# One factor of a gated recurrence, computed as (1 + a) times a root instead of as a root over (1 + a²)

## The chip, the cores and the metric

The kernel runs as one program on one core of a Trainium2 chip. The metric is the device time of one execution in microseconds; three executions of the kernel before are given, and their median counts. The engines are called TensorE (PE; PEld is its loading of weights), VectorE (DVE), ScalarE (ACT), GpSimd (POOL) and SyncE (SP), which here only issues DMAs.

## The reference

A model of two layers works on 256 context tokens and 256 latent tokens with 2048 features each. Every layer normalises, scales and shifts its input (`u`), multiplies it with one wide matrix `w_in`, gives the columns of the product to three mixers, and multiplies their gated results with `w_out`:

```
    u = rmsnorm(h, w) * (1 + scale) + shift
    lx, lg, q, k, v, ag, xbc, z, dt = split_cols(u @ w_in)
    h + gate * (concat([lru * silu(lg), att * silu(ag), ssd]) @ w_out)
```

`lru` is the mixer that the change is in, a gated linear recurrence over time, once forwards and once backwards, on 1024 columns; `att` is windowed attention with sinks; `ssd` is a chunked state-space mixer (Mamba-2), also in two directions. Of the recurrence, for one direction:

```
r = sigmoid(xc @ w_a + b_a);  i = sigmoid(xc @ w_x + b_x)      # xc: the column after a short convolution
log_a = -8 * r * softplus(-lambda)
a = exp(log_a)
b = sqrt(-expm1(2 * log_a)) * (i * xc)                         # sqrt(1 - a*a) * i * xc
h[t] = a[t] * h[t-1] + b[t]
```

## The kernel before, in words

**Projections.** Features lie on the 128 partitions, the 512 tokens in the free dimension. A projection's weights come in by DMA as pieces of four blocks of 128x128 (`raw`). ScalarE rounds a piece to TensorE's input format (`hi`, L237), VectorE subtracts that from the piece (`lo`, L238), and each block then takes three matmuls (`acc`, L174, called from `mm3`): `hi` with the rounded input, `hi` with the input's remainder, `lo` with the rounded input. So all three engines take part in every block, and TensorE works on blocks nearly all the time.

**The order of the work.** TensorE's order is fixed by the program as it is built: mixers are generators, and a planned clock that advances with each matmul says when a generator goes on (`spawn`, `pump`, and a table of waits by name and layer). The small matmuls of the mixers therefore stand among the blocks' matmuls at given places. All other engines are ordered by the compiler, which simulates a timeline and gives each engine a queue; a queue is worked off in order, and an instruction whose input is not ready holds up all behind it.

**The recurrence** (`lru_begin`, `lru_x`). There are eight column tiles `m` of 128 per layer, with two directions `d` each. For a tile, VectorE makes the convolution (`xc`, L466), ScalarE copies its halves over crosswise (`xsw`, L694), and TensorE multiplies with the gates' small matrices into two PSUM tiles (`mx`). ScalarE takes tanh of both with half the scale (L712, which frees the `mx` tiles; `lt0` is for r and `lt1` for i, since a sigmoid is (1 + tanh(z/2))/2). From `tr`, the tanh for r, come:

- L717: `tl` = tanh(log_a), where `s4` (-4 softplus) is both scale and bias, so that the argument is s4 (1 + tr) = log_a
- L718: `tr` becomes a = exp(log_a), in place
- L720: `a2` = a², a ScalarE square into a tile of its own (`la2`; the profile calls it `la`)
- L721: VectorE: `tl` = (1 + a²) tanh(log_a), which is a² - 1
- L722: VectorE: `ti` = (1 + ti) xc
- L724, once for both directions: `tl` = sqrt(-tl/16), in front of which ScalarE loads a table for the root
- L727, GpSimd, per direction: `ti` = `ti` times `tl`
- L730 (forwards), L733 and L735 (backwards, in two halves): the scans on VectorE; L739, GpSimd: the sum of the directions

**The state-space core.** Its steps run between those of the recurrence. `Output.begin` makes, per group of four heads, masked products (`cbm`, L1151), decays (`ee`: L1164 on ScalarE and L1165 on VectorE from `bc`, which a DMA broadcasts; the exponential at L1170), weights (`ww`, L1167 and L1168), their product (L1171), and `bc` likewise (L1175, L1176). `Output.end` multiplies `ee` with X and `bc` with the states H on TensorE into an `mx` tile and adds the result to Y (L1191, called X in the profile). The states are updated at L1119 to L1132.

**Tiles in rings.** Roles share buffers: `la2` is one of thirteen roles in a ring of four tiles of 128x512 (`xc`, the weighted X `xw` and the gates `lgt` are others). `mx` has four PSUM tiles, `acc` three.

Of the kernel before, what the change touches and what calls it, by code (L numbers as in the profile page):

```python
# [10 lines left out]
AF = mybir.ActivationFunctionType  # L11
ALU = mybir.AluOpType
AX = mybir.AxisListType

P = 128
# [124 lines left out]
class Kernel:  # L140
# [526 lines left out]
    def lru_begin(self, l):  # L667
        nc = self.nc
        o = PARAMS["lam"][0]
        ng = self.t([P, 16], "nlam", 1)  # L670
        nc.vector.tensor_scalar(out=ng, in0=self.prm[:, o:o + 16], scalar1=-1.0, scalar2=None, op0=ALU.mult)
        sp = self.softplus(ng, 16, "lsp")
        self.s4 = self.t([P, 16], "s4", 1)
        nc.vector.tensor_scalar(out=self.s4, in0=sp, scalar1=-4.0, scalar2=None, op0=ALU.mult)
        self.gb = self.t([P, 32], "gbh", 1)
        o = PARAMS["gab"][0]
        nc.vector.tensor_scalar(out=self.gb, in0=self.prm[:, o:o + 32], scalar1=0.5, scalar2=None, op0=ALU.mult)
        self.gws = [self.gate_weights(l, 0)]
        self.lruD = self.dram([8, P, 512], "lruD")
# [8 lines left out]
    def lru_x(self, l, m, px):  # L688
        nc = self.nc
        xc = self.t([P, 512], "xc")  # L690
        self.conv(xc, px, lambda tap: self.par("lcw", tap * 8 + m), self.par("lcb", m), 2)
        xs = self.t([P, 512], "xsw")
        for r, o in ((0, 64), (64, 0)):
            nc.scalar.activation(out=xs[r:r + 64], in_=xc[o:o + 64], func=AF.Copy)  # L694
        gw = self.gws.pop(0)
        if m < 7:
            self.gws.append(self.gate_weights(l, m + 1))
        yield self.wait("lx")
        ab = []
        tl = self.t([P, 2, 512], "ltl", 1)  # L700
        for d in range(2):
            if d:
                yield self.wait("lx2")
            th = []
            pg = [self.mx() for _ in range(2)]
            for r, c in ((0, 0), (64, 64), (0, 64), (64, 0)):
                x = xc if r == c else xs
                self.mm(pg[r // 64][c:c + 64], gw[r:r + 64, int(r != c), 2 * d + r // 64], x[r:r + 64], pos=(r, c),
                        side=4)
            for g in range(2):  # L710
                t = self.t([P, 512], f"lt{g}", 2)
                nc.scalar.activation(out=t, in_=pg[g], func=AF.Tanh, scale=0.5,  # L712
                                     bias=self.gb[:, 16 * g + 8 * d + m:16 * g + 8 * d + m + 1])
                th.append(t)
            tr, ti = th
            s4 = self.s4[:, 8 * d + m:8 * d + m + 1]
            nc.scalar.activation(out=tl[:, d], in_=tr, func=AF.Tanh, scale=s4, bias=s4)  # L717
            nc.scalar.activation(out=tr, in_=tr, func=AF.Exp, scale=s4, bias=s4)  # L718
            a2 = self.t([P, 512], "la2", 1)
            nc.scalar.activation(out=a2, in_=tr, func=AF.Square)  # L720
            nc.vector.scalar_tensor_tensor(out=tl[:, d], in0=a2, scalar=1.0, in1=tl[:, d], op0=ALU.add, op1=ALU.mult)  # L721
            nc.vector.scalar_tensor_tensor(out=ti, in0=ti, scalar=1.0, in1=xc, op0=ALU.add, op1=ALU.mult)  # L722
            ab.append((tr, ti))
        nc.scalar.activation(out=tl, in_=tl, func=AF.Sqrt, scale=-0.0625, bias=self.eps["s"])  # L724
        hs = []
        for d, (tr, ti) in enumerate(ab):
            nc.gpsimd.tensor_tensor(out=ti, in0=ti, in1=tl[:, d], op=ALU.mult)  # L727
            h = self.t([P, 512], f"lh{d}", 2)
            if d == 0:
                nc.vector.tensor_tensor_scan(out=h, data0=tr, data1=ti, initial=0.0, op0=ALU.mult, op1=ALU.add)  # L730
            else:
                r = lambda x, s: x[:, s:s + 256][:, ::-1]
                nc.vector.tensor_tensor_scan(out=r(h, 0), data0=r(tr, 0), data1=r(ti, 0), initial=0.0, op0=ALU.mult,  # L733
                                             op1=ALU.add)
                nc.vector.tensor_tensor_scan(out=r(h, C), data0=r(tr, C), data1=r(ti, C), initial=h[:, 0:1],  # L735
                                             op0=ALU.mult, op1=ALU.add)
            hs.append(h)
        s = C if l else 0
        nc.gpsimd.tensor_tensor(out=hs[0][:, s:], in0=hs[0][:, s:], in1=hs[1][:, s:], op=ALU.add)  # L739
        self.lru_h[m] = hs[0]  # L740
# [536 lines left out]
```

## Time and profile before

| what | value |
|---|---|
| three runs | 1833.20, 1832.97, 1830.13 us |
| median | 1832.97 us |
| the profiled execution | 1829.47 us |
| its span in the trace | 1827.5 us |
| mean granted TensorE clock | 0.991 |
| TensorE busy | 1765.5 us |

The profiled execution is one of its own, 3.5 us below the median; its span is the time from the first to the last record, and 2.0 us lie around it. The recurrence's tiles run at 240 to 500 us in the first layer and at 1255 to 1500 us in the second. Durations in the trace are those of one instruction, and successive ones on an engine overlap by about a tenth of a microsecond, so that what an instruction takes off an engine is a little less than its duration.

### The profile page before, as it was taken

How to read it: one execution, taken by the hardware profiler on the slowest of the kernel's cores; microseconds unless marked ns; L12 is line 12 of the kernel's file. 1: busy time of each engine (PE TensorE's matmuls, PEld its weight loads, DVE VectorE, ACT ScalarE, POOL GpSimd, SP SyncE). 2: the span in 40 equal slices, each digit the busy share in tenths (PEclk: the TensorE clock that was granted, in tenths of full speed). 3: DMA queues.
4: the chain of work that ended last, by engine and by line, in shares of the span. 5: the costliest groups of instructions: out<-in, count | busy, mean ns of one | idle time of the engine just before them, and what ended most of it. 6: DMA issues, size and time to landing. Idle time of an engine off the chain costs nothing.

```text
span 1827.5 us, 30170 instructions
## 1 busy us (share of the span) xinstructions
PE 1765.5 (97%) x10522; PEld 1453.4 (80%) x10522; DVE 1407.4 (77%) x3117; ACT 973.3 (53%) x1798; POOL 214.7 (12%) x179
## 2 busy tenths in 40 slices
PE   7999999999999999999999999999989999999999
PEld 4677876667778778887888887888767788999999
DVE  4447769898899778899999536877688785788665
ACT  4324578688523354556232235545688863678443
POOL 0000111111210021211000021010021130121000
PEclk9999999999999999999999999999999999999999
DMA  9982333434675545556766433455243564554655
GB/s 364 389 292 66 124 104 102 122 122 146 220 221 180 179 150 185 178 182 221 238 220 222 158 122 107 133 185 168 96 138 107 179 214 142 182 178 155 217 185 179
DMA packets 186344, 322.99 MB, mean 177 GB/s; under 512 B 19121, under 2 KB 44625, under 8 KB 185553
## 3 DMA queue, kind: packets, MB, share of 16 engines
q1 hardware_dynamic: 186192, 321.09, 54.2%
q8 instruction: 82, 1.34, 0.3%
q14 instruction: 70, 0.57, 0.1%
HBM read 310.38 MB, written 10.63 MB: 176 GB/s over the span
## 4 chain that ended last, share of the span: by engine, by line
PE 72%; DVE 9%; issue 7%; ACT 7%; DMA 3%; POOL 1%; SPq 0%; ACTq 0%; DVEq 0%; POOLq 0%
PE acc L174 55%; PE mx L174 13%; PE ada L174 3%; DVE lo L238 2%; PE mx L170 2%; DMA bc<-acsD 1%; ACT hi L237 1%; DVE ada L380 1%; DVE araw L380 1%; ACT lt L712 1%; DVE lh L730 1%; DMA araw<-in_adaw_dram 1%; DVE xc L466 1%; DVE ee L1165 1%; ACT ww L1167 1%
## 5 line engine op out<-in xcount | busy, mean ns | idle before, releaser
L174 PE MATMUL acc<-u,hi 128*128 128x512 f32 (+1 forms) x4800 | 1277.4, 355 | 3.9 <-ACT u L452 3.1
L174 PEld LDWEIGHTS acc<-u,hi 128*128 128x128 f32 x4800 | 837.1, 190 | 149.0 <-issue 32.6
L174 PE MATMUL acc<-u,lo 128*128 128x512 f32 (+1 forms) x2400 | 842.4, 351 | 6.9 <-DVE lo L238 6.7
L237 ACT ACTIVATE hi<-raw 128x512 fp32r<-128x512 f32 x640 | 397.8, 628 | 544.4 <-PE acc L174 420.8
L238 DVE TENSOR_TENSOR lo<-raw,hi 128x512 fp32r<-128x512 f32 x640 | 457.9, 718 | 184.6 <-ACT hi L237 172.7
L174 PEld LDWEIGHTS acc<-u,lo 128*128 128x128 f32 x2400 | 455.5, 190 | 71.9 <-DVE lo L238 11.7
L380 DVE SCALAR_TENSOR_TENSOR araw<-araw,adac 128x512 f32<-128x512 f32 x256 | 183.2, 716 | 6.9 <-DMA araw<-in_adaw_dram 4.1
L380 DVE SCALAR_TENSOR_TENSOR ada<-araw,adac 128x512 f32<-128x512 f32 x192 | 141.6, 738 | 13.0 <-DMA adac<-condD 7.0
L174 PE MATMUL mx<-u,hi 128*128 128x512 f32 (+1 forms) x320 | 99.7, 395 | 0.0
L1077 DVE SCALAR_TENSOR_TENSOR X<-acc,mod,X 128x256 f32<-128x256 f32 x144 | 65.0, 478 | 39.5 <-PE acc L174 39.4
L727 POOL TENSOR_TENSOR lt<-lt,ltl 128x512 f32<-128x512 f32 x32 | 45.5, 1443 | 326.2 <-ACT ltl L724 305.3
L868 POOL TENSOR_SCALAR prob<-prob,qrs 128x512 f32<-128x512 f32 (+1 forms) x48 | 58.2, 1227 | 214.7 <-ACT hi L237 124.7
L427 POOL TENSOR_TENSOR ssq<-ssq,sq 128x512 f32<-128x512 f32 (+1 forms) x26 | 34.1, 1312 | 308.0 <-ACT sq L423 308.0
L174 PEld LDWEIGHTS mx<-u,hi 128*128 128x128 f32 x320 | 56.6, 191 | 14.2 <-issue 4.6
L174 PE MATMUL mx<-u,lo 128*128 128x512 f32 (+1 forms) x160 | 61.0, 382 | 0.0
L511 POOL TENSOR_SCALAR X<-xs,prm 128x512 f32<-128x512 f32 (+1 forms) x16 | 15.4, 968 | 361.6 <-DVE xs L489 357.1
L174 PE MATMUL mx<-xc,gw 64*64 64x512 f32 x128 | 40.8, 619 | 8.9 <-ACT lt L712 5.9
L423 ACT ACTIVATE sq<-X 128x256 f32<-128x256 f32 (+1 forms) x44 | 18.8, 452 | 54.8 <-DVE X L654 53.1
L1165 DVE SCALAR_TENSOR_TENSOR ee<-bc,nacs,ee 128x128 f32<-128x128 f32 x96 | 35.9, 427 | 15.0 <-DMA bc<-acsD 9.6
L771 POOL TENSOR_TENSOR qw<-qw,cst 128x256 f32<-128x256 f32 x20 | 23.1, 1156 | 197.7 <-DVE rt L770 169.7
L712 ACT ACTIVATE lt<-mx,gbh 128x512 f32<-128x512 f32 x64 | 42.0, 674 | 4.1 <-PE mx L174 4.0
L1164 ACT ACTIVATE ee<-bc,nacs 128x128 f32<-128x128 f32 x96 | 30.9, 390 | 17.7 <-DMA bc<-acsD 17.7
(240 smaller groups left out, 1953.1 us busy)
## 6 DMA issues: line engine op xcount, KB each, us to landing
raw<-in_w_in_dram SPq DMA_DIRECT2D x448, 256.0 KB, 2.8
araw<-in_adaw_dram SPq DMA_DIRECT2D x256, 256.0 KB, 3.0
raw<-in_w_out_dram SPq DMA_DIRECT2D x192, 256.0 KB, 3.0
ar<-in_ada_dram SPq DMA_DIRECT2D x84, 256.0 KB, 5.4
bc<-acsD SPq DMA_DIRECT2D x48, 256.0 KB, 3.7
ar<-in_ada_dram SPq DMA_DIRECT2D x22, 512.0 KB, 6.9
adac<-condD SPq DMA_DIRECT2D x28, 256.0 KB, 4.5
gw<-in_gates_dram SPq DMA_DIRECT2D x16, 256.0 KB, 2.9
```

Source lines behind the costliest of these rows:

```text
L170: self.nc.tensor.transpose(out=out, in_=lhsT, identity=rhs)
L174: self.nc.tensor.matmul(out=out, lhsT=lhsT, rhs=rhs, start=start, stop=stop, **kw)
L237: nc.scalar.activation(out=hi, in_=part, func=AF.Copy)
L238: nc.vector.tensor_tensor(out=lo, in0=part, in1=hi.bitcast(F32), op=ALU.subtract)
L380: i = nc.vector.scalar_tensor_tensor(out=o, in0=raw, scalar=1.0, in1=row[c].rearrange("p t x -> p (t x)"), op0=ALU.mult, op1=ALU.mult, acc ...
L427: nc.gpsimd.tensor_tensor(out=self.ssq[0], in0=self.ssq[0], in1=sq, op=ALU.add)
L712: nc.scalar.activation(out=t, in_=pg[g], func=AF.Tanh, scale=0.5, bias=self.gb[:, 16 * g + 8 * d + m:16 * g + 8 * d + m + 1])
L727: nc.gpsimd.tensor_tensor(out=ti, in0=ti, in1=tl[:, d], op=ALU.mult)
L868: nc.gpsimd.tensor_scalar(out=pr[j], in0=pr[j], scalar1=rs[:, j:j + 1], scalar2=1.0, op0=ALU.mult, op1=ALU.mult)
L1077: nc.vector.scalar_tensor_tensor(out=x[:, s], in0=acc[:, s.start - w0:s.stop - w0], scalar=mod[:, 2 * KT + m, c:c + 1], in1=x[:, s], op0=A ...
L1164: nc.scalar.activation(out=e[:, j], in_=bcs[0][:, j], func=AF.Identity, bias=k.nacs[:, f:f + 1])
L1165: nc.vector.scalar_tensor_tensor(out=e[:, j], in0=bcs[1][:, j], scalar=k.nacs[:, r:r + 1], in1=e[:, j], op0=ALU.add, op1=ALU.min)
```

## The change

With T = tanh(log_a / 2) the identity sqrt(1 - a²) = (1 + a) sqrt(-T) is used in place of 1 - a² = -(1 + a²) tanh(log_a). A second scale `s2` of half the size is made once per layer. The square and its tile go; the multiply of VectorE stays in number, reads `a` in place of `a²`, and stands behind the root instead of ahead of it, once per direction and each just ahead of GpSimd's multiply. The root is still taken once for both directions. Behind the change, lines of `lru_x` up to the exponential have numbers higher by two: tanh of the gates is L714, the tanh 719, the exponential 720; VectorE's L722 becomes L721, the root L723, the multiply L726.

```
+        self.s2 = self.t([P, 16], "s2", 1)
+        nc.vector.tensor_scalar(out=self.s2, in0=sp, scalar1=-2.0, scalar2=None, op0=ALU.mult)
...
-            s4 = self.s4[:, 8 * d + m:8 * d + m + 1]
-            nc.scalar.activation(out=tl[:, d], in_=tr, func=AF.Tanh, scale=s4, bias=s4)
+            s4, s2 = (x[:, 8 * d + m:8 * d + m + 1] for x in (self.s4, self.s2))
+            nc.scalar.activation(out=tl[:, d], in_=tr, func=AF.Tanh, scale=s2, bias=s2)
             nc.scalar.activation(out=tr, in_=tr, func=AF.Exp, scale=s4, bias=s4)
-            a2 = self.t([P, 512], "la2", 1)
-            nc.scalar.activation(out=a2, in_=tr, func=AF.Square)
-            nc.vector.scalar_tensor_tensor(out=tl[:, d], in0=a2, scalar=1.0, in1=tl[:, d], op0=ALU.add, op1=ALU.mult)
             nc.vector.scalar_tensor_tensor(out=ti, in0=ti, scalar=1.0, in1=xc, op0=ALU.add, op1=ALU.mult)
...
         for d, (tr, ti) in enumerate(ab):
+            nc.vector.scalar_tensor_tensor(out=tl[:, d], in0=tr, scalar=1.0, in1=tl[:, d], op0=ALU.add, op1=ALU.mult)
             nc.gpsimd.tensor_tensor(out=ti, in0=ti, in1=tl[:, d], op=ALU.mult)
```

The orders of TensorE and of GpSimd are the same before and after. ScalarE has 32 instructions fewer, the squares, and 69 table loads either way; VectorE has two small ones more (`s2`, one per layer). In the orders that follow, a name is a tile with the number it got when it was made: `lt_592` before and `lt_590` after are the same tile, the second direction's `a`.

ScalarE before, in the second tile of the first layer, from the exponential of the second direction (L718) to the root (L724):

```order
L718 ACTIVATE lt_592_2838<-lt_592_2838,s_428_2078 128x512
L1164 ACTIVATE ee_2891<-bc_2887,nacs_2356 128x128 x4
L720 ACTIVATE la_594_2844<-lt_592_2838 128x512
L1167 ACTIVATE ww_2892<-cbm_2883,dt_2151 128x128 x4
L1167 ACTIVATE ww_2955<-cbm_2883,dt_2151 128x128 x4
L1175 ACTIVATE bc_2887<-bc_2887 128x512
L237 ACTIVATE hi_3037<-raw_3035 128x512
L1170 ACTIVATE ee_2891<-ee_2891 128x512
L724 ACT_TABLE_LOAD
L724 ACTIVATE ltl_2809<-ltl_2809,epss_92 128x1024
```

ScalarE after, the same place (exponential L720, root L723):

```order
L720 ACTIVATE lt_590_2833<-lt_590_2833,s_428_2078 128x512
L723 ACT_TABLE_LOAD
L723 ACTIVATE ltl_2807<-ltl_2807,epss_92 128x1024
L1164 ACTIVATE ee_2885<-bc_2881,nacs_2358 128x128 x4
L1167 ACTIVATE ww_2886<-cbm_2877,dt_2153 128x128 x4
L1167 ACTIVATE ww_2949<-cbm_2877,dt_2153 128x128 x4
L237 ACTIVATE hi_3031<-raw_3029 128x512
L1175 ACT_TABLE_LOAD
L1175 ACTIVATE bc_2881<-bc_2881 128x512
L1170 ACTIVATE ee_2885<-ee_2885 128x512
```

The table load and the root have moved up, past the steps of the state-space core, to right behind the exponential. A table load stands ahead of `bc`'s exponential (L1175) instead, since the root's table is in use until then.

VectorE before, the same place, from the first products `cbm` on:

```order
L1151 TENSOR_TENSOR cbm_2885<-mx_2881,cst_76 128x128
L1165 SCALAR_TENSOR_TENSOR ee_2891<-bc_2889,nacs_2356,ee_2891 128x128 x4
L721 SCALAR_TENSOR_TENSOR ltl_2809<-la_594_2844,ltl_2809 128x512
L1168 SCALAR_TENSOR_TENSOR ww_2892<-cbm_2885,dt_2151,ww_2892 128x128 x4
L1168 SCALAR_TENSOR_TENSOR ww_2955<-cbm_2885,dt_2151,ww_2955 128x128 x4
L1176 TENSOR_TENSOR bc_2887<-bc_2887,CT_1802 128x512
L238 TENSOR_TENSOR lo_3038<-raw_3035,hi_3037 128x512
L1191 TENSOR_TENSOR X_1805<-mx_2940,X_1805 128x2x128
L1171 TENSOR_TENSOR ee_2891<-ee_2891,ww_2892 128x512
```

VectorE after (L726 is the multiply behind the root):

```order
L1151 TENSOR_TENSOR cbm_2879<-mx_2875,cst_76 128x128
L726 SCALAR_TENSOR_TENSOR ltl_2807<-lt_586_2814,ltl_2807 128x512
L726 SCALAR_TENSOR_TENSOR ltl_2807<-lt_590_2833,ltl_2807 128x512
L1165 SCALAR_TENSOR_TENSOR ee_2885<-bc_2883,nacs_2358,ee_2885 128x128 x4
L1168 SCALAR_TENSOR_TENSOR ww_2886<-cbm_2879,dt_2153,ww_2886 128x128 x3
L730 SCALAR_TENSOR_TENSOR lh_592_2843<-lt_586_2814,lt_587_2816 128x512
L1168 SCALAR_TENSOR_TENSOR ww_2886<-cbm_2879,dt_2153,ww_2886 128x128
L1168 SCALAR_TENSOR_TENSOR ww_2949<-cbm_2879,dt_2153,ww_2949 128x128 x3
L733 SCALAR_TENSOR_TENSOR lh_593_2847<-lt_590_2833,lt_591_2835 128x256
L1168 SCALAR_TENSOR_TENSOR ww_2949<-cbm_2879,dt_2153,ww_2949 128x128
L238 TENSOR_TENSOR lo_3032<-raw_3029,hi_3031 128x512
L1176 TENSOR_TENSOR bc_2881<-bc_2881,CT_1802 128x512
```

Both multiplies stand one behind the other ahead of the decays `ee` (L1165), and the scans L730 and L733, which stood behind L1171 before, are among the weights `ww`. L1171 for `ee` follows three rows further on.

ScalarE before, in the last tile of the first layer, from the weights `ww` to the swapped halves `xsw`:

```order
L1164 ACTIVATE ee_4411<-bc_4407,nacs_2356 128x128 x4
L1167 ACTIVATE ww_4347<-cbm_4338,dt_2151 128x128 x4
L1167 ACTIVATE ww_4412<-cbm_4338,dt_2151 128x128 x4
L598 ACTIVATE spe_11776<-nlam_11774 128x16
L1175 ACTIVATE bc_4407<-bc_4407 128x512
L237 ACTIVATE hi_4541<-raw_4539 128x512
L694 ACTIVATE xsw_4301<-xc_4296 64x512 x2
```

ScalarE after, the same place:

```order
L1164 ACTIVATE ee_4389<-bc_4385,nacs_2358 128x128 x4
L696 ACTIVATE xsw_4279<-xc_4274 64x512 x2
L1167 ACTIVATE ww_4325<-cbm_4316,dt_2153 128x128 x4
L1167 ACTIVATE ww_4390<-cbm_4316,dt_2153 128x128 x4
L598 ACTIVATE spe_11746<-nlam_11744 128x16
L1175 ACTIVATE bc_4385<-bc_4385 128x512
```

The two copies to `xsw` stand ahead of the eight weights instead of behind them.

## Rows read from the trace of the kernel before

**Rows 1.** The page: engines, then the chain that ended last, by engine.

```profile
PE 1765.5 (97%) x10522; PEld 1453.4 (80%) x10522; DVE 1407.4 (77%) x3117; ACT 973.3 (53%) x1798; POOL 214.7 (12%) x179
...
PE 72%; DVE 9%; issue 7%; ACT 7%; DMA 3%; POOL 1%; SPq 0%; ACTq 0%; DVEq 0%; POOLq 0%
```

**Rows 2.** Busy us by engine (count), TensorE clock, DMA share, GB/s, of two stretches.

```profile
360.00:420.00 60.00, 55.53 (x303) 39.69 (x301) 55.32 (x112) 47.39 (x100) 8.28 (x6) 1.00 0.35 113
420.00:480.00 60.00, 57.59 (x298) 42.83 (x297) 55.49 (x123) 41.48 (x73) 11.12 (x8) 0.97 0.59 200
```

**Rows 3.** TensorE's waits, 222 to 500 us: total, times, longest.

```profile
PE mx L174 <- DVE ee L1171: 4.5, 2, 3.1
PE mx L174 <- ACT lt L712: 3.1, 1, 3.1
PE mx L174 <- DVE H L1132: 2.7, 1, 2.7
PE mx L174 <- ACT xsw L694: 2.3, 1, 2.3
```

**Rows 4.** TensorE's waits, 1225 to 1500 us.

```profile
PE mx L174 <- ACT lt L712: 9.7, 7, 4.1
PE acc L174 <- DVE lo L238: 4.7, 5, 1.6
```

**Rows 5.** Groups by form: count | busy, mean ns | idle before, releaser.

```profile
L238 DVE TENSOR_TENSOR lo<-raw,hi 128x512 fp32r<-128x512 f32 x640 | 457.9, 718 | 184.6 <-ACT hi L237 172.7 <-DMA ar<-in_ada_dram 5.5 <-PE acc L174 2.0
...
L727 POOL TENSOR_TENSOR lt<-lt,ltl 128x512 f32<-128x512 f32 x32 | 45.5, 1443 | 326.2 <-ACT ltl L724 305.3 <-DVE X L1191 20.9
...
L730 DVE TENSOR_TENSOR_SCAN lh<-lt,lt 128x512 f32<-128x512 f32 x16 | 29.0, 1813 | 8.9 <-POOL lt L727 8.9
...
L724 ACT ACT_TABLE_LOAD x16 | 20.5, 1283 | 0.3
...
L720 ACT ACTIVATE la<-lt 128x512 f32<-128x512 f32 x32 | 20.0, 628 | 0.6
...
L724 ACT ACTIVATE ltl<-ltl,epss 128x1024 f32<-128x1024 f32 x16 | 18.4, 1153 | 0.2
...
L733 DVE TENSOR_TENSOR_SCAN lh<-lt,lt 128x256 f32<-128x256 f32 x16 | 10.7, 672 | 0.0
```

**Rows 6.** ScalarE's waits, 222 to 500 us.

```profile
ACT xsw L694 <- DVE xc L466: 14.2, 5, 4.2
...
ACT ee L1164 <- DMA bc<-acsD: 8.7, 5, 2.7
```

**Rows 7.** VectorE's waits, 222 to 500 us.

```profile
DVE ltl L721 <- ACT la L720: 2.1, 4, 0.7
```

**Rows 8.** Timeline of ScalarE, second LRU tile: start us, us, operation [idle].

```profile
274.50 0.80 ACT L718 ACTIVATE lt<-lt,s 128x512 f32<-128x512 f32 x1
```

**Rows 9.** Timeline of VectorE, same stretch.

```profile
275.97 1.13 DVE L1165 SCALAR_TENSOR_TENSOR ee<-bc,nacs,ee 128x128 f32<-128x128 f32 x4
...
281.44 0.68 DVE L1171 TENSOR_TENSOR ee<-ee,ww 128x512 f32<-128x512 f32 x1
...
283.92 1.35 DVE L238 TENSOR_TENSOR lo<-raw,hi 128x512 fp32r<-128x512 f32 x1 [1.20 <-ACT hi L237]
```

**Rows 10.** Timeline of TensorE, around the second tile's SSD outputs.

```profile
283.89 0.45 PE L174 MATMUL mx<-ee,X 128*64 128x128 f32 x4
...
293.20 0.70 PE L174 MATMUL mx<-ee,X 128*64 128x128 f32 x4 [3.15 <-DVE ee L1171]
```

**Rows 11.** Busy time and clock of two short stretches.

```profile
292.40:299.20 6.80, 6.00 (x26) 4.84 (x27) 6.80 (x12) 2.74 (x8) 2.55 (x2) 0.50 0.19 67
...
442.60:446.00 3.40, 3.33 (x25) 2.91 (x24) 3.40 (x8) 3.31 (x7) 0.00 (x0) 0.50 0.57 178
```

**Rows 12.** Timeline of ScalarE, around 440 and 1415 us.

```profile
440.38 1.28 ACT L694 ACTIVATE xsw<-xc 64x512 f32<-64x512 f32 x2
...
1415.60 1.28 ACT L1175 ACT_TABLE_LOAD   x1
```

## The prediction, made before the changed kernel was run

> **What bounds the kernel now.** I read the page's engines first, then the chain, then a table of stretches, and only then waits and timelines. TensorE is busy for 97% of the span and leads the chain with 72%; VectorE (77% busy, 9% of the chain) and ScalarE (53%, 7%) come in only where TensorE waits for them [rows 1]. A ScalarE instruction less is therefore worth nothing by itself; it is worth what it takes out of TensorE's waits. The change lies in the recurrence's tiles, so the stretch decides, not the average: from 360 to 480 us VectorE is busy for 55.32 + 55.49 = 110.8 of 120 us, as close to the limit as TensorE (113.1), while ScalarE is busy for 88.9 [rows 2]. Here VectorE is the second engine at its limit, and ScalarE is not. TensorE's waits in the stretch are few and single: 4.5 us in two for `ee`'s product (L1171), 3.1 us in one for the gates' tanh, 2.7 us for H, 2.3 us for `xsw` [rows 3]; in the second layer 9.7 us in seven for the tanh and 4.7 us in five for `lo` [rows 4]. These sums, 12.6 and 14.4 us, are nearly all there is to gain. Some waits cost more than their length: behind that of 3.15 us [rows 10] the clock stands at 0.50 (1.2 GHz) for 6.8 us, and behind the one for `xsw` for 3.4 us [rows 11], which with TensorE busy in nearly all of it costs half of each, 3.4 and 1.7 us.
>
> **The change part by part.**
>
> *The squares.* Thirty-two of 628 ns, 20.0 us in all, leave ScalarE [rows 5]; since successive instructions overlap by a tenth, some 0.53 us each, 17 us. All of it lies beside TensorE's matmuls. VectorE waited for the squares for only 2.1 us in four times, at most 0.7 [rows 7], so even VectorE gains little from their going. Directly: 0. If the cover were gone, that is if ScalarE set the pace, it would be up to 17 us.
>
> *The second scale.* Two VectorE operations on 128x16, once per layer. No row shows their like alone; the nearest is the half scan of 128x256 at 672 ns [rows 5], so from 0 to 1.3 us on both, ahead of the first tiles. I take 0, for TensorE is in the projections there and VectorE is not at its limit. The tanh and the exponential keep their shapes, so 0.
>
> *The ring.* The square's tile no longer goes round in the ring of four. The squares idled 0.6 us in all before they started [rows 5], so they waited for no tile. The other roles of the ring may get theirs earlier, which is a gain from 0 to the 14.2 us that `xsw` waited for `xc` on ScalarE in the first layer [rows 6]. I take 0 for it: what stands ahead of `xc` on VectorE is other VectorE work.
>
> *The root moves up and VectorE's multiply moves behind it.* This is the part with a price. The multiply could run when the square was done; now it needs a table load (1283 ns) and a root of 1153 ns, 2.43 us, against 0.53 to 0.63 us for the last square. VectorE works its queue off in order, and behind the multiply stand `ee`, `ww` and L1171, for which TensorE has stood still before. In the second tile of the first layer I follow it through. The exponential starts at 274.50 and ends at 275.30 [rows 8], so load and root end at 275.30 + 2.43 = 277.7. VectorE reached `ee` (L1165) at 275.97 [rows 9]; now both multiplies stand ahead of it, so it idles 277.7 - 276.0 = 1.7 us. Ahead of L1171 there come further one multiply more (0.6), the scan L730 (0.5 to 1.8: its mean, 1813 ns, holds the longer ones beside GpSimd) and the half scan L733 (0.67) [rows 5], some 3.1 at most, and GpSimd's two multiplies of 1443 ns, which now lie beside all this: a `lo` in the shadow of one took 1.35 us [rows 9] against a mean of 0.72 [rows 5], and I put that down as 1.7 us on the stretch. L1171 ended at 281.44 + 0.68 = 282.1; now at 282.1 + 1.7 + 3.1 + 1.7 = 288.6. TensorE wanted it at 283.89 and did not wait [rows 10]: there was 1.8 us of slack, and there will be a wait of 288.6 - 283.9 = 4.7 us. For the next output, where it waited 3.15, the scans are now out of the way, and 0.6 us remain. Sum for the tile: 4.7 + 0.6 - 3.15 = +2.15 us. The clock falls once before and once after, so 0 for that. A second tile of the first layer has the same root ahead of the same product; its wait, 2.43 less a few tenths of slack, I take as +2.1 us. For the other six I take 0: there the root is done before VectorE comes to the multiply. Bounds: from 0 (root always in time) to 8 tiles by 1.7, 13.6 us; between them I stand at 4.25, nearest to the tile worked out.
>
> *ScalarE's other work shifts.* Moved up with the root, a few instructions of 0.53 us now stand ahead of the gates' tanh at two places, one in each layer: two each, +1.05 and +1.05, together +2.1 us. In the other direction: the second wait for L1171 (4.5 - 3.1 = 1.4) goes, -1.35. In the last tile of the first layer the copies to `xsw` ran at 440.38, behind eight weights [rows 12]; they stand ahead of them now, so of the wait of 2.3 us at least 0.9 goes, and with a wait of 1.4 I take it that the clock keeps its level (from 360 to 420 us, where the waits of 1.4 and 2.7 us lie, it is 1.00 throughout [rows 2, 3]), so -0.9 - 1.7 = -2.6. In the second layer, a table load of 1.28 us at 1415.60 [rows 12] no longer stands ahead of a tanh for which TensorE waits, and another wait is shorter by a square: -2.1. The longest wait there, 4.1 us, ended with a `bc` whose DMA stood behind a weight's on SyncE and does not any more: -1.0. Of the `lo` waits I take a square per two, -1.0. Bounds for these gains: 0, and all of rows 3 and 4, 27 us, less the waits for H.
>
> *Sum.* +4.25 + 2.1 - 1.35 - 2.6 - 2.1 - 1.0 - 1.0 = -1.7 us. From the profiled execution, 1829.47, that gives 1827.8; the runs' median is 3.5 us above that execution, so I add 3.5 and predict 1831 us. Against the median it is -0.1%. About 0.2%, 3.7 us, is what a measurement of this kernel tells from no change; the sum is under it.
>
> **GpSimd beside VectorE.** The row is the one above: a `lo` with two inputs in SBUF took 1.35 us while GpSimd multiplied, against 0.72 in the mean [rows 5, 9]. The Trainium skill, page "SBUF — State Buffer", section "Who interferes with whom", has a rule for it: a VectorE instruction with two SBUF inputs and a GpSimd instruction that reads SBUF take one pair of ports for a whole instruction, and the one that comes second waits for all of the other. That speaks against this change, since the second direction's multiply now stands in the queue exactly when GpSimd starts on the first direction's. By the rule it would wait for up to 1.44 us, sixteen times; by the row it would lose 0.63 us, sixteen times. In the sum neither stands: GpSimd multiplies 32 times before and after, and whichever VectorE instruction lies beside it pays.
>
> **The rivals.**
>
> *ScalarE's relief reaches TensorE (faster).* The waits for the tanh are 3.1 + 9.7 = 12.8 us [rows 3, 4], and 17 us leave ScalarE. If the tanh comes earlier at all of these places, the time is 1829.47 - 12.8 + 3.5 = 1820.2; at half of them, 1826.6. For it: the tanh is the second layer's largest wait. Against: ScalarE itself waits, 14.2 us for `xc` and 8.7 us for the DMA of `bc` in the first layer [rows 6]; time taken off ahead of such a wait only lengthens it, and the squares stand behind the tanh of their own tile.
>
> *VectorE is held by the root (slower).* One mechanism: a multiply at the head of VectorE's queue waits for table and root, and everything behind it comes late to TensorE. It decides where VectorE has less than the 1.8 us of slack that the second tile shows. Over 360 to 480 us it idles for 9.2 us, with four tiles in it [rows 2]. If four tiles pay 1.7 us and no gain elsewhere comes, the time is 1829.47 + 6.8 + 3.5 = 1839.8; with all eight, 13.6 us, 1846.6. By the rule on the ports each would add up to 1.44 us, the same rival and not one of its own. Against it: the compiler's order put the multiplies behind some other work in most tiles.
>
> *The change is not what moves the time.* The queues of ScalarE, VectorE and SyncE are made anew by the compiler, and what differs is mainly their order; table loads stay at 69. Then the time may come out anywhere within a few microseconds, 1833 in the middle.
>
> **How the numbers follow.** Waits trade places, the forecast: 0.52, with its own range from 1826 to 1837; of it 0.33 within 0.2%, 0.12 faster, 0.07 slower. ScalarE's relief: 0.22, all faster. VectorE held: 0.20, of it 0.18 slower and 0.02 within. Only the order: 0.06, with 0.02 faster, 0.03 within, 0.01 slower. Together: faster 0.36, within 0.38, slower 0.26. The range goes from the full relief, 1820, to just above four tiles held, 1842.
>
> **What would show it.** Right: in the profile after, ScalarE has 32 operations and some 20 us less in the recurrence; TensorE's waits there sum to about what they did, with a longer one for L1171's output near 284 us, and none or a short one for `xsw` near 440. VectorE's list of waits has a new row, the multiply for the root, of 1 to 2 us a time. Wrong to the fast side: the tanh's waits in the second layer fall below half of 9.7 us. Wrong to the slow side: the multiply waits for the root in most of the tiles and L1171 is late in more than two, or VectorE's longer operations beside GpSimd rise in number. If the waits are as now and the time differs, the clock's low stretches have to show it.

## The result: slower by 1.1%

| | median us | runs | ratio to before, 95% interval |
|---|---|---|---|
| before | 1831.55 | 4 (1829.46 to 1833.20) | |
| changed | 1851.98 | 4 (1845.10 to 1854.22) | 1.0108 [1.0093, 1.0123] |

The changed kernel takes 20 us more; the forecast was 1831, with a range to 1842. Its profiled execution took 1853.59 us, with a span of 1851.6, 24.1 us more than the one before.

The page of the changed kernel, the engines and the chain, beside [rows 1]:

```profile
PE 1777.0 (96%) x10522; PEld 1461.5 (79%) x10522; DVE 1412.1 (76%) x3119; ACT 959.5 (52%) x1766; POOL 221.4 (12%) x179
...
PE 76%; DVE 9%; ACT 8%; DMA 4%; issue 3%; POOL 0%; SPq 0%; ACTq 0%; DVEq 0%; POOLq 0%
```

ScalarE has its 32 squares less (1766 operations against 1798), and 13.8 us less to do. The time shows none of it: TensorE has the same 10522 matmuls and is busy for 11.5 us more, which goes with the lower clock (below), and the rest is waiting.

TensorE's waits in the first and the second layer's recurrence (in total, times, longest), from 222 to 520 and from 1225 to 1540 us, beside [rows 3] and [rows 4]; in these somewhat longer stretches the rows before that are compared here have the same numbers:

```profile
PE mx L174 <- DVE ee L1171: 9.5, 5, 4.4
PE mx L174 <- ACT lt L714: 4.1, 2, 3.8
```

```profile
PE acc L174 <- DVE lo L238: 9.1, 6, 2.0
PE mx L174 <- ACT lt L714: 7.9, 5, 3.9
PE acc L174 <- ACT hi L237: 5.0, 4, 1.9
```

In the first layer the waits for L1171's product are five instead of two, 9.5 us against 4.5. In the second the tanh's waits are shorter, 7.9 against 9.7, as ScalarE's relief would have it; but the waits for `lo` have doubled from 4.7 to 9.1 us, and waits for `hi`, of which there was none before, make 5.0. VectorE's list has the new row that the prediction named, here for both layers:

```profile
DVE ltl L726 <- ACT ltl L723: 13.5, 8, 2.5
```

```profile
DVE ltl L726 <- ACT ltl L723: 12.3, 8, 2.5
```

Sixteen waits, once per tile, 25.8 us in all. The clock, beside [rows 11], in two stretches of the second layer (columns as there):

```profile
1447.60:1454.40 6.80, 5.09 (x14) 3.67 (x15) 6.80 (x9) 4.79 (x10) 2.80 (x2) 0.50 0.35 115
1502.20:1509.00 6.80, 5.77 (x27) 5.77 (x28) 6.80 (x10) 3.01 (x5) 2.12 (x2) 0.50 0.50 162
```

TensorE's gaps of more than 0.3 us and the time at a clock of 0.50, summed over the trace's records for the two profiled executions:

| | gaps before | gaps after | clock at 0.50 before | after |
|---|---|---|---|---|
| 222 to 520 us | 14.2 | 19.8 | 13.7 | 13.7 |
| 1225 to 1540 us | 15.6 | 23.4 | 3.4 | 23.9 |
| all | 56.3 | 68.9 | 35.4 | 61.4 |

Twelve and a half microseconds more of gaps, and 26 us more at half the clock, worth 13: 25.6 us for the span's 24.1. Since TensorE's order is the same in both, its instructions can be laid side by side one by one: the changed kernel is 0.9 us behind at 240 us of the one before, 5.8 at 490, 8.3 at 1225 and still at 1300, and 23.7 at 1530. So a third of the loss lies in the first layer and two thirds in the second, where the prediction had seen a gain.

**What happens in the second layer.** ScalarE, VectorE and GpSimd of the changed kernel at the first of the places (start us, us, operation, [idle before]):

```profile
1328.45 0.81 ACT L720 ACTIVATE lt<-lt,s 128x512 f32<-128x512 f32 x1
1329.26 1.28 ACT L723 ACT_TABLE_LOAD   x1
1330.55 1.15 ACT L723 ACTIVATE ltl<-ltl,epss 128x1024 f32<-128x1024 f32 x1
1331.61 0.61 ACT L237 ACTIVATE hi<-raw 128x512 fp32r<-128x512 f32 x1
1332.13 0.76 ACT L460 ACTIVATE xc<-acc,prm 128x512 f32<-128x512 f32 x1
```

```profile
1331.73 1.29 DVE L726 SCALAR_TENSOR_TENSOR ltl<-lt,ltl 128x512 f32<-128x512 f32 x2 [1.86 <-ACT ltl L723]
1332.94 1.76 DVE L238 TENSOR_TENSOR lo<-raw,hi 128x512 fp32r<-128x512 f32 x1
```

```profile
1332.51 3.34 POOL L727 TENSOR_TENSOR lt<-lt,ltl 128x512 f32<-128x512 f32 x2 [11.28 <-DVE ltl L726]
```

And TensorE there:

```profile
1332.27 0.51 PE L174 MATMUL acc<-u,hi 128*128 128x256 f32 x2 [1.67 <-ACT hi L237]
1334.76 0.41 PE L174 MATMUL acc<-u,lo 128*128 128x256 f32 x1 [1.98 <-DVE lo L238]
```

Table load and root stand right behind the exponential, and the next `hi` behind them, 2.4 us of load and root later: TensorE waits 1.67 us for it. VectorE has nothing to do in the meantime but its multiplies, since `lo` needs `hi`, and waits 1.86 us for the root; then it runs both, 1.29 us, ahead of `lo`. The first multiply's end starts GpSimd, and `lo` lies beside it and takes 1.76 us. TensorE waits another 1.98 us for that `lo`. Before, at this place:

```profile
1320.73 0.81 ACT L718 ACTIVATE lt<-lt,s 128x512 f32<-128x512 f32 x1
1321.57 0.63 ACT L720 ACTIVATE la<-lt 128x512 f32<-128x512 f32 x1
1322.11 0.76 ACT L460 ACTIVATE xc<-acc,prm 128x512 f32<-128x512 f32 x1
1322.77 1.14 ACT L237 ACTIVATE hi<-raw 128x512 fp32r<-128x512 f32 x2
1323.93 1.28 ACT L724 ACT_TABLE_LOAD   x1
1325.22 1.15 ACT L724 ACTIVATE ltl<-ltl,epss 128x1024 f32<-128x1024 f32 x1
```

```profile
1322.24 0.69 DVE L721 SCALAR_TENSOR_TENSOR ltl<-la,ltl 128x512 f32<-128x512 f32 x1
...
1323.57 0.68 DVE L238 TENSOR_TENSOR lo<-raw,hi 128x512 fp32r<-128x512 f32 x1
...
1324.83 0.68 DVE L238 TENSOR_TENSOR lo<-raw,hi 128x512 fp32r<-128x512 f32 x1
```

The compiler's queue had `xc` and two `hi` between the square and the table load, while VectorE did its multiply; VectorE made both `lo` of them around ScalarE's table load, and TensorE did not wait at all here. The same pair of waits, for `hi` and then for `lo`, comes again at 1447, 1475 and 1501 us, and at or just behind each of the four a stretch at a clock of 0.50 begins (1335.0, 1447.6, 1478.3 and 1502.2 us).

### The profile page after: what moved, and what is told of

It is laid out like the page before. It is cut to its first block, busy times and chain, and to the rows that moved or that the text cites. A ratio compares the mean times of both kernels' runs of the same rounds, so it can differ in the third digit from the quotient of the medians.

```text
span 1851.6 us, 30124 instructions
## 1 busy us (share of the span) xinstructions
PE 1777.0 (96%) x10522; PEld 1461.5 (79%) x10522; DVE 1412.1 (76%) x3119; ACT 959.5 (52%) x1766; POOL 221.4 (12%) x179
## 4 chain that ended last, share of the span: by engine, by line
PE 76%; DVE 9%; ACT 8%; DMA 4%; issue 3%; POOL 0%; SPq 0%; ACTq 0%; DVEq 0%; POOLq 0%
PE acc L174 59%; PE mx L174 13%; DVE lo L238 3%; PE ada L174 3%; DMA bc<-acsD 2%; PE mx L170 2%; ACT lt L714 1%; ACT ww L1167 1%; DMA araw<-in_adaw_dram 1%; DVE ada L380 1%; DVE araw L380 1%; ACT lt L720 1%; ACT L723 1%; ACT ltl L719 1%; ACT hi L237 1%
## 5 line engine op out<-in xcount | busy, mean ns | idle before, releaser
L238 DVE TENSOR_TENSOR lo<-raw,hi 128x512 fp32r<-128x512 f32 x640 | 470.3, 738 | 182.5 <-ACT hi L237 169.6
L727 POOL TENSOR_TENSOR lt<-lt,ltl 128x512 f32<-128x512 f32 x32 | 52.5, 1658 | 312.6 <-DVE ltl L726 312.6
L868 POOL TENSOR_SCALAR prob<-prob,qrs 128x512 f32<-128x512 f32 (+1 forms) x48 | 58.1, 1225 | 214.8 <-ACT hi L237 124.2
L511 POOL TENSOR_SCALAR X<-xs,prm 128x512 f32<-128x512 f32 (+1 forms) x16 | 15.4, 965 | 362.6 <-DVE xs L489 358.1
L1165 DVE SCALAR_TENSOR_TENSOR ee<-bc,nacs,ee 128x128 f32<-128x128 f32 x96 | 35.8, 423 | 23.6 <-DMA bc<-acsD 20.7
L714 ACT ACTIVATE lt<-mx,gbh 128x512 f32<-128x512 f32 x64 | 41.9, 674 | 9.0 <-PE mx L174 9.0
```

Of the source, the lines that this page charges most:

```text
L238: nc.vector.tensor_tensor(out=lo, in0=part, in1=hi.bitcast(F32), op=ALU.subtract)
L868: nc.gpsimd.tensor_scalar(out=pr[j], in0=pr[j], scalar1=rs[:, j:j + 1], scalar2=1.0, op0=ALU.mult, op1=ALU.mult)
L1165: nc.vector.scalar_tensor_tensor(out=e[:, j], in0=bcs[1][:, j], scalar=k.nacs[:, r:r + 1], in1=e[:, j], op0=ALU.add, op1=ALU.min)
```

## The experiments

Every kernel was timed beside the kernel before on the same chip. Theory A: the multiply behind the root. B: the missing square. C: VectorE beside GpSimd. D: the root's place on ScalarE, formed after the first four runs.

| kernel | median us | ratio to before, 95% interval |
|---|---|---|
| e1_late_square | 1851.67 | 1.0119 [1.0103, 1.0135] |
| e2_no_square | 1824.71 | 0.9966 [0.9953, 0.9978] |
| e3_early | 1839.95 | 1.0055 [1.0040, 1.0070] |
| e4_tiny | 1847.59 | 1.0101 [1.0085, 1.0116] |
| f1_early_gate | 1830.93 | 1.0003 [0.9991, 1.0014] |
| f2_after_gate | 1833.63 | 1.0024 [1.0012, 1.0037] |
| f3_early_gate_once | 1831.18 | 1.0008 [0.9997, 1.0019] |
| f4_wide_one_input | 1843.63 | 1.0079 [1.0062, 1.0095] |
| g0_gate_layer0 | 1847.94 | 1.0097 [1.0076, 1.0118] |
| g1_gate_layer1 | 1837.41 | 1.0030 [1.0015, 1.0045] |
| h1_gpsimd_square | 1824.96 | 0.9967 [0.9954, 0.9980] |
| h2_direct | 1823.79 | 0.9964 [0.9953, 0.9975] |

**The change in its two halves.** e1_late_square does the move alone, e2_no_square the removal alone, both from the kernel before:

```
 e1: - stt(tl, in0=a2, 1.0, in1=tl)        # ahead of the root
     + stt(tl, in0=a2, 1.0, in1=tl)        # behind it, ahead of GpSimd's multiply
 e2: - a2 = tile("la2"); activation(a2, tr, Square)
     - stt(tl, in0=a2, 1.0, in1=tl)
     + stt(tl, in0=tr, 1.0, in1=tl)
```

> The kernel before, with the square kept and VectorE's multiply by (1 + a squared) moved behind the root (the root is then taken of -tanh alone, so this kernel's factor is another one than the reference's). Theory A, the multiply behind the root: VectorE waits at the head of its queue for table load and root, and ScalarE's root is moved ahead of other work; the time is that of the changed kernel or a little more, 1848 to 1858 us. Theory B, the missing square: taking 32 squares out made the compiler order the queues anew and worse; here they are in, so 1828 to 1836 us. Theory C, VectorE's multiply now lies beside GpSimd's and they block each other: as A, 1848 to 1858.

> The kernel before without the square; VectorE's multiply stays ahead of the root and reads a in place of a squared (the square is left out, so the factor is another one than the reference's). Theory A: nothing waits for the root but GpSimd, as before, and the time is that of before or some microseconds less, 1824 to 1834 us. Theory B: 1846 to 1856, as the changed kernel. Theory C: as A.

The move alone costs 21 us, as much as the change; the removal alone gains 6. B has fallen: the square's going is the good half. e1 is as slow as the changed kernel, but its waits lie elsewhere: 11.9 us for L1171's product in the first layer (the changed kernel 9.5), in the second 7.0 for `lo` (9.1) and only 1.4 for `hi` (5.0).

**The identity without the move.** e3_early multiplies (1 + a) into `ti` ahead of the root; e4_tiny adds a step behind the root that only has to wait:

```
 e3: - stt(tl, in0=tr, 1.0, in1=tl)        # behind the root
     + stt(ti, in0=tr, 1.0, in1=ti)        # ahead of it
 e4: e3, and behind the root, ahead of GpSimd's multiply:
     + vector.tensor_scalar(tl[:, d, 0:1], tl[:, d, 0:1], 1.0, mult)
```

> The changed kernel's identity with (1 + a) multiplied into ti ahead of the root, not into the root's result: as many VectorE operations as in the changed kernel, none of them behind the root. Theory A: 1824 to 1834 us, the loss of 20 us is gone. Theory B: 1846 to 1856. Theory C: 1824 to 1834.

> As the kernel with (1 + a) multiplied into ti, with a VectorE operation on one column (128x1, times 1.0) behind the root for each direction, ahead of GpSimd's multiply, where the changed kernel has its multiply. Theory A: the wait for the root at the head of VectorE's queue is the cost, so the time is near that of the changed kernel, 1844 to 1856 us, though the operation itself has next to no work. Theory C: the operation reads one tile and lasts a tenth of the multiply, so 1826 to 1838. Theory B: 1846 to 1856.

e4 does as A says: a step of 148 ns that waits for the root costs 7.6 us over e3. But e3 is a miss for all three theories. Nothing of VectorE stands behind its root, and still it loses 10 us against before and 15 against e2, which has as many operations but for `s2`. Two things differ: the multiply stands on `ti` and not on the root's input (theory E, below), and the root waits for something else. In the kernel before and in e2 VectorE's multiply lies between tanh and root; in e3, as in the changed kernel, the root follows ScalarE's own tanh, and the queue has it right behind the exponential:

```profile
1321.45 0.81 ACT L720 ACTIVATE lt<-lt,s 128x512 f32<-128x512 f32 x1
1322.28 1.28 ACT L724 ACT_TABLE_LOAD   x1
1323.58 1.15 ACT L724 ACTIVATE ltl<-ltl,epss 128x1024 f32<-128x1024 f32 x1
1324.63 0.61 ACT L237 ACTIVATE hi<-raw 128x512 fp32r<-128x512 f32 x1
```

So it is in all sixteen tiles of the changed kernel and of e1, e3, e4 and f4: in the trace no other ScalarE work lies between the last exponential and the table load. In the kernel before some does in all sixteen, in e2, f1, f2 and f3 in fifteen.

**The root's place alone.** Theory D says that this place is the main cost. To put the root back without giving VectorE anything to wait for, a one-column step of VectorE goes in front of it, which changes no value:

```
     activation(tr, tr, Exp, scale=s4, bias=s4)
   + vector.stt(tl[:, d, 0:1], in0=tr[:, 0:1], 0.0, in1=tl[:, d, 0:1], mult, add)
 f1: in e3_early          f2: in the changed kernel
 f3: as f1, for d = 1     g0, g1: as f2, in the first or the second layer only
```

> As e3_early, but in front of the root a VectorE operation on one column (128x1; it adds zero times a to the tanh) for each direction, so that the root again comes behind VectorE as in the kernel before. Theory D, the root's place on ScalarE: without a VectorE step between tanh and root the compiler puts table load and root right behind the exponential, ahead of hi, ee and ww, and e3_early's 15 us over e2_no_square are this; so 1822 to 1831 us here. Theory E, e3_early's loss is that the second multiply stands on ti, ahead of the scans and next to other VectorE work: 1836 to 1844 us.

> The changed kernel with the same one-column VectorE operations in front of the root; its multiplies stay behind the root. If the root's place (15 us by e3_early against e2_no_square) and the multiply behind the root (12 us by the changed kernel against e3_early) are two costs that add up, 1833 to 1841 us. If VectorE's wait behind the root is what costs and the root's place does not matter once VectorE waits for it, 1848 to 1856 us.

> As f1_early_gate with the one-column operation for the second direction alone, half as many of them. Theory D: 1821 to 1831 us. Theory E: 1836 to 1844 us.

f1 and f3 are level with the kernel before, at the upper end of D's range (f3 a fifth of a microsecond over it). So of e3's 15 us over e2 the root's place is some 9 or 10. f1, which has no square either, is still 0.37%, 7 us, above e2. The number of one-column steps is not the reason, since f3 has half of them and is no faster; the second multiply on `ti` (theory E) may be, and no run takes it out. f2 is the telling run: the changed kernel with all of its multiplies behind the root, and 32 steps of 157 ns more, is back at 1.0024. About 15 us of the 20 (1.0108 - 1.0024 = 0.84%) go with a step that does nothing but come before the root. It lies at the low end of what two costs that add up would give. Taken from f1, the root's place alone (e3) is 0.52%, the multiply behind the root alone (f2) 0.21%, together 0.73%; both at once (the changed kernel) are 1.05%. So they cost more together than one by one, by 0.32%; with the intervals of 0.11 to 0.15% on each of the four ratios that difference is itself uncertain by some 0.27%: it is likely there, and its size is open. ScalarE and VectorE of f2 at the place shown above:

```profile
1324.57 0.81 ACT L720 ACTIVATE lt<-lt,s 128x512 f32<-128x512 f32 x1
1325.28 0.61 ACT L237 ACTIVATE hi<-raw 128x512 fp32r<-128x512 f32 x1
1325.80 0.76 ACT L460 ACTIVATE xc<-acc,prm 128x512 f32<-128x512 f32 x1
1326.46 0.62 ACT L237 ACTIVATE hi<-raw 128x512 fp32r<-128x512 f32 x1
1327.10 1.28 ACT L724 ACT_TABLE_LOAD   x1
1328.39 1.15 ACT L724 ACTIVATE ltl<-ltl,epss 128x1024 f32<-128x1024 f32 x1
```

```profile
1325.98 0.69 DVE L238 TENSOR_TENSOR lo<-raw,hi 128x512 fp32r<-128x512 f32 x1
...
1327.26 0.68 DVE L238 TENSOR_TENSOR lo<-raw,hi 128x512 fp32r<-128x512 f32 x1
...
1329.58 1.29 DVE L727 SCALAR_TENSOR_TENSOR ltl<-lt,ltl 128x512 f32<-128x512 f32 x2 [0.98 <-ACT ltl L724]
```

Two `hi` and `xc` are ahead of the table load again and two `lo` ahead of the multiplies. VectorE still waits for the root, 0.98 us here, and in both layers 14 times, 17.7 us in all (the changed kernel 16 times, 25.8): the step in front of the root shortens this wait too. In the second layer TensorE's wait for `hi` falls from 5.0 to 0.2 us and that for `lo` from 9.1 to 6.5. The waits in f2's second layer:

```profile
DVE ltl L727 <- ACT ltl L724: 5.9, 6, 1.7
```

```profile
PE mx L174 <- ACT lt L714: 7.7, 5, 4.2
PE acc L174 <- DVE lo L238: 6.5, 6, 1.8
...
PE acc L174 <- ACT hi L237: 0.2, 1, 0.2
```

> The changed kernel with the one-column operations in front of the root in the first layer only. By the traces the changed kernel is some 7 us behind in the first layer and 16 us in the second (of 24 in all). If the root's place costs in each layer by itself (theory D), the first layer's part goes and the second's stays: 1843 to 1849 us. If one place decides, about 1834 or about 1852.

> The same in the second layer only. Theory D, layer by layer: the second layer's part goes, 1835 to 1841 us. If one place decides, about 1834 or about 1852.

Both came inside what D gives layer by layer. The second layer's root is worth 1.0108 - 1.0030 = 0.78%, 14 us, the first layer's 0.11%, 2 us, and within its interval perhaps nothing; together 16, near f2's 15.

**GpSimd.** f4_wide_one_input widens e4's step to all columns, with one input; h1_gpsimd_square, from the kernel before, makes the square on GpSimd:

```
 f4: tensor_scalar(tl[:, d], tl[:, d], 1.0, mult)          # instead of [:, d, 0:1]
 h1: - scalar.activation(a2, tr, Square)
     + gpsimd.tensor_tensor(a2, tr, tr, mult)
```

> As e4_tiny, with the operation behind the root over all 512 columns: one input in SBUF and a number, where the changed kernel's multiply has two inputs. If the changed kernel's last 4 us over e4_tiny are the operation's width, which delays what stands behind it, 1849 to 1855 us. If they come from its second input, by blocking against GpSimd, 1844 to 1849 us.

> The kernel before, with the square made by GpSimd instead of ScalarE. ScalarE loses the 32 squares as in e2_no_square, VectorE's operations stay the same in number and ahead of the root; 32 GpSimd multiplies more lie beside VectorE. If VectorE operations beside GpSimd's are what costs (theory C), 1836 to 1850 us; if not, 1824 to 1832.

f4 came just below both ranges, 4 us faster than the narrow step, about as much as the two intervals leave open; its step takes 423 ns, where the changed kernel's multiply with two inputs takes 689. Width is not the cost; whether the second input is, this can't say, since the two kernels' queues differ too. h1 settles more: with 32 GpSimd multiplies more beside VectorE it is faster than before. Its rows, with one of the kernel before ahead of them:

```profile
L721 DVE SCALAR_TENSOR_TENSOR ltl<-la,ltl 128x512 f32<-128x512 f32 x32 | 21.9, 687 | 5.2 <-ACT la L720 5.0
```

```profile
L238 DVE TENSOR_TENSOR lo<-raw,hi 128x512 fp32r<-128x512 f32 x640 | 461.1, 723 | 177.4 <-ACT hi L237 163.8 <-DMA ar<-in_ada_dram 5.2 <-DMA araw<-in_adaw_dram 2.0
...
L720 POOL TENSOR_TENSOR la<-lt 128x512 f32<-128x512 f32 x32 | 39.1, 1222 | 225.7 <-ACT lt L718 183.0 <-DVE lt L722 19.0 <-PE acc L174 14.9
...
L721 DVE SCALAR_TENSOR_TENSOR ltl<-la,ltl 128x512 f32<-128x512 f32 x32 | 24.1, 752 | 5.2 <-POOL la L720 5.2
```

GpSimd's square takes 1222 ns, and VectorE's multiply 752 against 687 before the edit, `lo` 723 against 718 [rows 5]. Being beside GpSimd costs VectorE some microseconds in sum; C as the cause of all 20 us has fallen. f2 says the same: GpSimd's multiplies take 1690 ns in it and 1658 in the changed kernel, against 1443 before [rows 5], and f2 loses 4 us. A part C has: at the four places of the second layer the `lo` that TensorE waits for is one that GpSimd's multiplies lengthen. What that part is worth, no run takes out.

**A direct factor.** h2_direct, from the kernel before, drops tanh and square and lets VectorE square a:

```
 h2: - activation(tl, tr, Tanh);  activation(a2, tr, Square);  stt(tl, a2, 1.0, tl)
     + vector.tensor_tensor(tl[:, d], tr, tr, mult)        # root of 0.0625 (1 - tl) + floor
```

> The kernel before with the factor taken straight from the root of 1 - a squared: VectorE squares a where its multiply stood, ahead of the root, and both the tanh and the square of ScalarE go (less exact near a = 1, with a floor of a millionth under the root). Theory D and the gain of e2_no_square: nothing but GpSimd waits behind the root, and ScalarE has 64 operations, some 40 us, less: 1817 to 1826 us. If ScalarE's relief is not worth more than the square's: 1823 to 1831.

It came where either expectation allows, level with e2 and h1. Thirty-two ScalarE operations more are gone than in e2, and the time is the same within the intervals, so as far as these kernels show, what ScalarE's relief can give here is used up at 6 to 7 us.

The kernels faster than both are e2, h1 and h2; of them h1 computes the kernel before's formula unchanged, at 0.9967 [0.9954, 0.9980].

## Why the prediction was wrong

*What held.* Most of ScalarE's time is off the path: the squares' going is worth 6 us by e2, where the sum had 0 for it directly and 17 as the bound. VectorE waits for the root: in the second tile of the first layer it idles for 1.65 us (worked out: 1.7), and TensorE's wait there is 4.38 us (worked out: 4.7):

```profile
279.83 1.29 DVE L726 SCALAR_TENSOR_TENSOR ltl<-lt,ltl 128x512 f32<-128x512 f32 x2 [1.65 <-ACT ltl L723]
```

```profile
290.92 0.70 PE L174 MATMUL mx<-ee,X 128*64 128x128 f32 x4 [4.38 <-DVE ee L1171]
```

The sum for this tile came out nearer than its parts, which is in part luck. GpSimd's shadow fell on `ee` and cost 2.1 us (3.20 against 1.13 [rows 9]; worked out for all of the stretch: 1.7), the further multiply and the scans cost some 2.3 (worked out: 3.1 at most), and a step on H (0.6), which no term had, came ahead of L1171:

```profile
281.04 3.20 DVE L1165 SCALAR_TENSOR_TENSOR ee<-bc,nacs,ee 128x128 f32<-128x128 f32 x4
```

For the next output 0.92 us are left (worked out: 0.6). The `xsw` copies came ahead of the weights, and their wait is gone.

*The step that failed* is "For the other six I take 0: there the root is done before VectorE comes to the multiply", and with it the silence on the second layer. VectorE waited for the root in all sixteen tiles, 1.6 us each in the mean. This part stood in the sum at +4.25 us, all of it in the first layer. By layer, the terms of the sum make +1.35 us for the first and -3.05 for the second; laid side by side, TensorE fell back by 7.4 us in the first and by 15.4 in the second. The order of the second layer's queues was read for the tanh only; there the root had moved past `hi` and `xc`, and these rows were to be had. The prediction followed who waits for VectorE, and of ScalarE's shifted work only the tanh, `xsw` and `bc`; it never asked who waits for what now stands behind the root. That was the larger question: by g1, the second layer's root back in its place is worth 14 us of the 20. Not all of the 14 need be `hi`: with the root in its place VectorE's wait for it is shorter as well, 5.9 us in f2's second layer against 12.3.

*The rivals.* "VectorE is held by the root" had the sign and a chance of 0.20, and of the places only the first layer's. Its price, 6.8 to 13.6 us, counted a wait per tile and no clock; in the second layer the loss is a `hi` and a `lo` late in a row, and about as much again from the clock, which fell at each such pair. And VectorE held behind the root alone is not enough: f2 has it, 17.7 us of it, and loses 0.24%. The first rival, ScalarE's relief, is right in half of its size (6 of 12.8 us), but not by its way: TensorE's waits for the tanh are 11.9 us in e2 [rows 3, 4: 12.8]. Whether the ports were rightly left out of the sum is open. VectorE's busy time rises by only 4.7 us in all, but single instructions on the path are longer, `ee` above and the four `lo`. At the first place both multiplies ran in 1.29 us, the second not blocked (2 x 0.69 less the overlap) and under way before GpSimd's began; GpSimd's two took 3.34 us where they had 3.00, and `lo` behind them 1.76. By the rule of the Trainium skill, page "SBUF — State Buffer", section "Who interferes with whom", a VectorE instruction with two SBUF inputs that comes second to a GpSimd instruction that reads SBUF waits until that one is done. That agrees: `lo` began 0.43 us after GpSimd's first multiply (1332.94 against 1332.51), so of that one's 1.67 us, half of the pair, some 1.2 were left, and `lo` lost 1.1. The size of 0.63 us used in the prediction was too small for this place.

*What stays open.* Over f1, e3's early root costs some 10 us, f2's multiply behind the root 4, and the two together 19. The places shown (`hi` late, then the multiplies, then GpSimd beside `lo`) are the changed kernel's. e3's profiled execution hardly has them: TensorE's waits for `hi` are small there and those for `lo` are 4.2 us in the second layer, against 4.7 in f1; those for L1171's product in the first layer are more than double f1's, and those for the tanh in the second 11.5 us against 9.9. In e3's first and second layer:

```profile
PE mx L174 <- DVE ee L1171: 9.7, 3, 5.7
```

```profile
PE acc L174 <- ACT hi L237: 1.7, 3, 0.8
```

and in f1's first (where L1172 is that product):

```profile
PE mx L174 <- DVE ee L1172: 4.3, 1, 4.3
```

That the root's place and the multiply behind it make the loss is shown by taking each out; by which waits each does so alone, and why the two cost more together, was not taken apart further. Of the first layer's 7 us only 2 came back by the times of g0, whose interval allows for more; laid side by side, its profiled execution is 4.5 us behind at 1225 us, where the changed kernel is 8.3. Why the compiler puts a root that depends on ScalarE alone at the front was not tried.

## What to carry to other kernels

Before moving a step behind another, ask what it kept apart: the multiply between tanh and root was also what held the root and its table load back, while ScalarE served TensorE. On a queue worked off in order, it is no gain that an instruction can run earlier if it is then placed ahead of work that others wait for; look for who stands behind it on its own engine, not only for who waits for its result. And read the order in every stage that repeats the pattern: the same edit put TensorE back by 7 us in one layer and by 15 in the other, and the root's old place was worth 2 us in the one and 14 in the other.

## What the runs showed of the hardware

The clock about doubled the damage. In the second layer TensorE's gaps grew by 7.8 us, and the time at a clock of 0.50 by 20.5 us, worth about 10. Four pairs of waits of 2.7 to 3.7 us (`hi` and `lo` together) had four stretches of 3.4 to 6.8 us at 0.50 with them, where before the change one wait of 4.1 us left one, of 3.4 us. A VectorE `lo` right behind the start of GpSimd's pair of multiplies took 1.76 us at two of these places, and three of them 4.05 us at the other two (1475 and 1501 us), against 0.72 for one in the mean before [rows 5]. A VectorE step on one column costs 148 ns (e4, a product with a number) and 157 ns (f2, with two inputs).
